# Issuing the down-product weight fetches from GpSimd's queue instead of SyncE's

## The chip, the cores and the metric

The kernel runs on one core of one Trainium2 chip. The metric is the device time of one execution in microseconds (us). Five engines work side by side: TensorE (PE, matmuls, with PEld for its weight loads), VectorE (DVE), ScalarE (ACT), GpSimd (POOL) and SyncE (SP). Data moves between device memory and the on-chip buffers by DMA. A DMA is issued by one of the engines' instruction queues: the queue waits in order, first for the semaphores of the instruction at its head, then issues it; 16 DMA engines carry the transfer out, and a semaphore tells when it has landed.

## The reference

Two layers, each a half-step SwiGLU, a mixing block and a second half-step SwiGLU, on 512 tokens of width 1024; all in float32. The change concerns the last matrix product of the SwiGLU, `@ w_down`, whose inner size D_FF is 2816 (22 tiles of 128):

```python
def _swiglu(t, w_gate, w_up, w_down):
    return (jax.nn.silu(t @ w_gate) * (t @ w_up)) @ w_down

for l in range(DEPTH):
    f = _swiglu(_rmsnorm(h, ffn1_pre_g[l]), ffn1_w_gate[l], ffn1_w_up[l], ffn1_w_down[l])
    h = h + 0.5 * _rmsnorm(f, ffn1_post_g[l])
    ...
    f = _swiglu(_rmsnorm(h, ffn2_pre_g[l]), ffn2_w_gate[l], ffn2_w_up[l], ffn2_w_down[l])
    h = h + 0.5 * _rmsnorm(f, ffn2_post_g[l])
```

## The kernel before

**Precision.** Every float32 operand is split into a high part (ScalarE's cast, line 182) and a low part (VectorE's subtraction, line 183), and each product is three matmuls: high by high, high by low, low by high (lines 205 to 207 in `mm3`). One weight block of a `Unit` is two tiles of 128 rows by 512 columns, 512 KB. It is fetched into a raw buffer, split into `wh` and `wl`, and then feeds 12 matmuls of 128x512.

**The seven products.** In the four feed-forwards (two layers, `a` before and `c` after the mixing) 16 of the 22 tiles of D_FF go through a scheme of seven products in the place of eight (Strassen's, in Winograd's form): `token_products` for the gate and up matrices and `products()` for the down matrix. Down has two chunks `ci` of eight tiles, each with seven products `n`, in the order of `DOWN`, which makes 14 jobs of two units each. `BLOCKS` says which quarter of the weights a product reads. Products 2, 3, 5 and 6 need a sum of quarters: VectorE subtracts the fetched block and a kept one (line 327, tile `bt`, made by `keep`). Product 2 fetches both quarters; product 4 takes over the raw block of product 3 and fetches nothing. The other six tiles of D_FF go through `down()`, whose blocks are plain `Unit`s.

**The order of the work.** The host program `Queue` walks a list of jobs, laid out by `PLAN`, in which the down jobs alternate with gate and up jobs of the last four tiles (kinds `g` and `u`). `Queue.load_ahead` splits the blocks of the following jobs, four units ahead; each time a block has been split, `loaded()` calls `fetch_ahead()`, which issues the next fetches in the order of the jobs until the ring that the next unit's place belongs to is full. In the down stage there are two `raw` buffers, shared with the gate and up blocks, and two buffers of the ring `o`. The framework's planner then lays out each engine's instructions, mostly in the order of the program, sets the semaphores, and may let an instruction pass another on its queue that is not ready; `keep_in_program_order` forbids this for one instruction.

**The queues.** SP's queue issues nearly every transfer of the kernel: the plain `Unit` fetches (line 249), the block fetches of `BlockUnit.block` (line 297), the transposes of `turn()` (line 808), the gain rows (line 136), the saving and bringing back of the residual, and the output. POOL's queue carries three small vectors (lines 122, 123 and 156) and some copies and memsets of the mixing, among them the tile `cut` (lines 1161 and 1164).

**What a block fetch waits for.** Its instruction waits at the head of its queue until the buffer's last reader is done, which is a VectorE instruction of line 183 or 327.

Of the kernel before, what the change touches and what calls it, by code (L numbers as in the profile page):

```python
# [18 lines left out]
P = 128  # L19
# [4 lines left out]
def kernel(  # L24
# [38 lines left out]
    nc = tc.nc  # L63
# [40 lines left out]
    def stile(shape, tag, name, dt=F32R):  # L104
        return sb.tile(shape, dt, tag=tag, bufs=BUFS[tag], name=name)
# [126 lines left out]
    class Unit:  # L232


        def __init__(self, src, k0, nk, c0, ncol, name, scale=None):
            self.tags, self.place = ("wh", "wl"), "raw"
            self.src, self.k0, self.nk, self.c0, self.ncol, self.name, self.scale = src, k0, nk, c0, ncol, name, scale
            self.h = self.raw = None
# [35 lines left out]
    class BlockUnit(Unit):  # L274
# [9 lines left out]
        def __init__(self, n, src, rows, k0, nk, ncol, keep, name, place="raw"):  # L284
            super().__init__(src, k0, nk, 0, ncol, name)
            self.n, self.rows, self.keep, self.fetched, self.place = n, rows, keep, False, place
            self.heir, self.behind = None, False

        def inherits(self, un):
            un.heir, self.place = self, None  # L290
# [3 lines left out]

        def block(self, dst, b):
            r = (b[0] * self.rows + self.k0) * P
            return nc.sync.dma_start(dst, self.src[r:r + self.nk * P, b[1] * self.ncol:(b[1] + 1) * self.ncol]
                                     .rearrange("(k p) c -> p k c", p=P))

        def fetch(self):  # L300
# [309 lines left out]
    def ffn(l, src, wg, wu, wd, dst, name, spare, parked, plan, aside=None):  # L610
# [89 lines left out]
        def sums():  # L700
# [4 lines left out]
            def fp32(i, j):  # L705
                t = whole(f"x{i}{j}")
                tt(t, block(i, j, 0).bitcast(F32), block(i, j, 1).bitcast(F32), ALU.add)
                return t
# [16 lines left out]
            yield "S2"  # L725
            tt(x11, x11, x21, ALU.subtract)
            tt(s, block(0, 1, 0).bitcast(F32), s, ALU.subtract)
            yield "S3"
            tt(s, s, block(0, 1, 1).bitcast(F32), ALU.add)
            pair(4, s)  # L730
            yield "S4"
# [126 lines left out]
        def product(at, uns):  # L858
            ci, n = DOWN[at]
            first, last = ci == 0, ci == NC - 1  # L860
            if at == 0:
                RINGS["o"] = 2
                dst.begin()
            if at + 1 < len(DOWN):
                first_factor(*DOWN[at + 1])
            if first and n in (0, 2):
                st["b", SUM[n]] = [pbank("z", f"pd{name}_{n}_{e}") for e in range(2)]
            pts = st["b", SUM[n]]
            h, l = st.pop(("a", ci, n))
            opens, ends = first and n in (0, 2), last and n in (1, 4, 6)  # L870
            for un in uns:
                for e in range(2):
                    c = slice(e * P, (e + 1) * P)
                    for k in range(un.nk):
                        kk = un.k0 + k
                        mm3(pts[e][:], h[:, kk, c], l[:, kk, c], un.h[:, k], un.l[:, k], opens and kk == 0,
                            ends and kk == FC // 2 - 1, free=True)
                        yield 3 * S * PE_US
                    turn(un.k0 + e)
            if not last:  # L880
                return
            if n == 0:
                st["b", 1] = [pbank("z", f"pd{name}_1_{e}") for e in range(2)]
                for e in range(2):
                    nc.scalar.copy(st["b", 1][e][:], pts[e][:])
                return
            i, hf = TO[n]
            for e in range(2):
                f = dst.fs[2 * i + e][:, HF[hf]]
                if n in (4, 5):  # L890
                    nc.vector.tensor_tensor(f, f, pts[e][:], ALU.add)
                else:
                    nc.scalar.copy(f, pts[e][:])

        def products():

            keep = [Keep(lambda k0, ci=ci: stile([P, 2, S], "o", f"bt{name}_{ci}_{k0}", F32)[:]) for ci in range(NC)]
            had = {}
            for at, (ci, n) in enumerate(DOWN):
                w = wd[l, ci * FC * P:(ci + 1) * FC * P]  # L900
                uns = [BlockUnit(n, w, FC // 2, k, 2, S, keep[ci], f"d{name}_{ci}_{n}_{k}", ("raw", "o")[k // 2])
                       for k in range(0, FC // 2, 2)]
                for un in uns:
                    un.behind = n == 2
                if n == 4:
                    for un, of in zip(uns, had[ci, 3]):
                        un.inherits(of)
                had[ci, n] = uns
                yield uns, (lambda at=at, uns=uns: product(at, uns))
# [18 lines left out]
        def queue(what):  # L928
            kind, n = what[0], what[1]
            if kind in "gu":  # L930
                if n not in made:
                    made[n] = plain(n)
                ms = (what[2],) if what[-1] in (0, 1) and len(what) == 3 else range(2)
                uns = made[n][kind == "u"]
                run = (lambda: gates(n, uns, ms)) if kind == "g" else (lambda: ups(n, uns, ms))
                Q.add(uns if ms[0] == 0 else [], run)
            elif kind == "a":
                Q.add([], lambda: iter(first_factor(n, 0) or ()))
            elif kind == "m":
                if name == "a0":  # L940
                    Q.add([], mem_stats)
            else:
                if what not in made:
                    made[what] = products() if kind == "d" else token_products(n, kind == "U")
                for one in made[what]:
                    Q.add(*one)
                    break
# [775 lines left out]
```

## Time and profile before

| | us |
|---|---|
| median of 3 runs | 2356.36 (2354.06 to 2357.69) |
| the profiled execution | 2354.76 |
| its span, first to last instruction | 2353.0 |
| VectorE busy in the span | 1798.8 |
| ScalarE busy in the span | 1505.3 |
| POOL busy in the span | 75.5 |

The granted clock of TensorE is 0.999 of full speed over the profiled execution. The profile is read in five views, and each row names its engine, its line in the kernel, the operation, and the tiles as "out<-in" without their buffer numbers:

- the page: the busy time of each engine, the chain of work that ended last, and the groups of transfers with the median time from issue to landing
- the busy time of each engine in stretches of the span
- the waits: who waited for whom, with the sum, the count and the longest
- the instructions on one tile, with their durations and, for transfers, the quickest, median and slowest landing
- the timeline of one engine: start, length, the instruction, and in brackets how long the engine stood idle before it and what ended that

"SPq" marks an issue on SP's queue. A PE instruction's end is modelled, so matmuls overlap in the timeline.

### The profile page before, as it was taken

Reading aid. Unit: us, or ns where it says so; the run is one execution under the profiler, and the core shown is the slowest. Engines: PE = TensorE matmul, PEld = TensorE weight load, DVE = VectorE, ACT = ScalarE, POOL = GpSimd, SP = SyncE. Lnnn points to the kernel's source line nnn. Section 1 sums busy time; section 2 is a strip of 40 time slices with the busy share of each in tenths; the row PEclk is TensorE's granted clock in tenths of the full one; section 3 lists DMA queues with packets and bytes.
Section 4 is the critical chain, followed back from the end, with each engine's and each line's share of the span. In section 5 each row is a group of like instructions: output and inputs, shape, how many; then the busy total and the mean of one; then the engine's idle time right before and its main releaser. Section 6 shows DMA issues by size and latency. Waiting matters only on the chain.

```text
span 2353.0 us, 30931 instructions
## 1 busy us (share of the span) xinstructions
PE 2339.6 (99%) x11623; PEld 1977.7 (84%) x11623; DVE 1798.8 (76%) x2359; ACT 1505.3 (64%) x2302; POOL 75.5 (3%) x134
## 2 busy tenths in 40 slices
PE   9999999999999999999999999999999999999998
PEld 7888888888888888878898888888888888988887
DVE  8877876577777688878798788766677767888785
ACT  6677465576766556774656774655777665667744
POOL 0000000000111000000000000000001100000000
PEclk9999999999999999999999999999999999999999
DMA  6667454223323555674646655532323235566744
GB/s 206 192 178 220 143 197 129 78 83 88 91 72 108 188 188 159 199 188 153 225 145 182 202 176 178 189 108 72 100 72 99 73 124 190 170 189 181 207 145 146
DMA packets 297849, 354.96 MB, mean 151 GB/s; under 512 B 78282, under 2 KB 189154, under 8 KB 297700
## 3 DMA queue, kind: packets, MB, share of 16 engines
q1 hardware_dynamic: 297604, 352.97, 48.8%
q8 instruction: 91, 1.49, 0.3%
q14 instruction: 58, 0.48, 0.1%
q0 software_dynamic: 96, 0.03, 0.0%
HBM read 319.39 MB, written 16.78 MB: 143 GB/s over the span
## 4 chain that ended last, share of the span: by engine, by line
PE 90%; DMA 4%; DVE 2%; ACT 2%; issue 1%; SPq 0%; DVEq 0%; ACTq 0%
PE pg L206 4%; PE pg L205 4%; PE pg L207 4%; PE pda L206 3%; PE pdc L206 3%; PE pda L205 3%; PE pda L207 3%; PE pdc L207 3%; PE pdc L205 3%; PE pb L207 1%; PE pb L206 1%; PE pb L205 1%; PE pq L205 1%; PE pq L206 1%; PE pk L207 1%
## 5 line engine op out<-in xcount | busy, mean ns | idle before, releaser
L205 PE MATMUL pg<-us_a,wh_wg 128*128 128x512 f32 x384 | 151.1, 394 | 0.0
L206 PE MATMUL pg<-us_a,wh_wg 128*128 128x512 f32 x384 | 149.9, 390 | 0.0
L207 PE MATMUL pg<-us_a,wl_wg 128*128 128x512 f32 x384 | 149.9, 390 | 0.0
L183 DVE TENSOR_TENSOR wl_da<-raw_da,wh_da 128x1024 fp32r<-128x1024 f32 x50 | 61.0, 1224 | 46.3 <-ACT wh_da L182 46.1
L183 DVE TENSOR_TENSOR wl_dc<-raw_dc,wh_dc 128x1024 fp32r<-128x1024 f32 x50 | 61.0, 1223 | 44.5 <-ACT wh_dc L182 44.4
L206 PE MATMUL pdc<-wl_dc,ahc 128*128 128x512 f32 x224 | 88.0, 393 | 1.5 <-DVE wl_dc L183 1.5
L206 PE MATMUL pda<-wl_da,aha 128*128 128x512 f32 x224 | 88.0, 393 | 0.3 <-DVE wl_da L183 0.3
L207 PE MATMUL pdc<-wh_dc,alc 128*128 128x512 f32 x224 | 87.3, 390 | 0.0
L207 PE MATMUL pda<-wh_da,ala 128*128 128x512 f32 x224 | 87.3, 390 | 0.0
L205 PE MATMUL pdc<-wh_dc,ahc 128*128 128x512 f32 x224 | 86.7, 390 | 0.4 <-ACT wh_dc L182 0.4
L205 PE MATMUL pda<-wh_da,aha 128*128 128x512 f32 x224 | 86.6, 390 | 0.0
L207 PEld LDWEIGHTS pg<-us_a,wl_wg 128*128 128x128 f32 x384 | 72.1, 188 | 15.1
L205 PEld LDWEIGHTS pg<-us_a,wh_wg 128*128 128x128 f32 x384 | 72.2, 188 | 14.1
L206 PEld LDWEIGHTS pg<-us_a,wh_wg 128*128 128x128 f32 x384 | 72.2, 188 | 14.0
L182 ACT CAST wh_da<-raw_da 128x1024 fp32r<-128x1024 f32 x50 | 52.2, 1049 | 41.5 <-DMA raw_da<-in_ffn_w_down_dram 13.6
L182 ACT CAST wh_dc<-raw_dc 128x1024 fp32r<-128x1024 f32 x50 | 52.1, 1049 | 36.5 <-DMA raw_dc<-in_ffn_w_down_dram 12.2
L186 DVE SCALAR_TENSOR_TENSOR wl_wg<-raw_wg,wh_wg 128x1024 fp32r<-128x1024 f32 x48 | 58.5, 1222 | 21.9 <-ACT wh_wg L185 21.8
L200 DVE SCALAR_TENSOR_TENSOR ga<-pg,bgate,ga 128x512 f32<-128x512 f32 x48 | 35.9, 747 | 50.0 <-ACT ga L199 50.0
L182 ACT CAST wh_uc<-raw_uc 128x1024 fp32r<-128x1024 f32 x44 | 46.3, 1053 | 39.8 <-PE pwc0g L207 9.4
L183 DVE TENSOR_TENSOR wl_uc<-raw_uc,wh_uc 128x1024 fp32r<-128x1024 f32 x44 | 53.7, 1221 | 17.1 <-ACT wh_uc L182 16.9
L185 ACT ACTIVATE wh_wg<-raw_wg 128x1024 fp32r<-128x1024 f32 x48 | 50.5, 1056 | 25.1 <-PE pv L1113 11.7
L182 ACT CAST wh_ua<-raw_ua 128x1024 fp32r<-128x1024 f32 x44 | 46.2, 1052 | 31.1 <-PE pwa0g L207 8.1
(643 smaller groups left out, 8017.3 us busy)
## 6 DMA issues: line engine op xcount, KB each, us to landing
raw_da<-in_ffn_w_down_dram SPq DMA_DIRECT2D x66, 512.0 KB, 4.7
raw_dc<-in_ffn_w_down_dram SPq DMA_DIRECT2D x66, 512.0 KB, 4.3
raw_ga<-in_ffn_w_gate_dram SPq DMA_DIRECT2D x52, 512.0 KB, 4.5
raw_ua<-in_ffn_w_up_dram SPq DMA_DIRECT2D x52, 512.0 KB, 4.7
raw_gc<-in_ffn_w_gate_dram SPq DMA_DIRECT2D x52, 512.0 KB, 4.0
raw_uc<-in_ffn_w_up_dram SPq DMA_DIRECT2D x52, 512.0 KB, 4.0
raw_wg<-in_w_gate_dram SPq DMA_DIRECT2D x48, 512.0 KB, 3.6
raw_wo<-in_w_out_dram SPq DMA_DIRECT2D x24, 512.0 KB, 3.4
```

Of the source, the lines that this page charges most:

```text
L182: both = [nc.scalar.copy(h_ap, src)]
L183: make = lambda: nc.vector.tensor_tensor(l_ap, src, h_ap.bitcast(F32), ALU.subtract)
L185: both = [nc.scalar.activation(h_ap, src, AF.Copy, scale=scale)]
L186: make = lambda: nc.vector.scalar_tensor_tensor(l_ap, src, scale, h_ap.bitcast(F32), ALU.mult, ALU.subtract)
L200: nc.vector.scalar_tensor_tensor(t, z, minus, t, ALU.max, ALU.add)
L205: nc.tensor.matmul(pt, lh, rh, start=start, stop=False, skip_group_check=free)
L206: nc.tensor.matmul(pt, lh, rl, start=False, stop=False, skip_group_check=free)
L207: nc.tensor.matmul(pt, ll, rh, start=False, stop=stop, skip_group_check=free)
```

## The change

`BlockUnit` gets an attribute `queue`, by default SyncE's, and `block()` issues its DMA there. `products()` sets it to GpSimd's for all units of the 14 down jobs. This covers the raw fetches and the fetches of the kept blocks of product 2, which stay pinned in program order. The gate and up products, the plain units of `down()` and everything else stay with SyncE.

```diff
@@ class BlockUnit, __init__
-            self.heir, self.behind = None, False
+            self.heir, self.behind, self.queue = None, False, nc.sync
@@ class BlockUnit, block
-            return nc.sync.dma_start(dst, self.src[r:r + self.nk * P, b[1] * self.ncol:(b[1] + 1) * self.ncol]
+            return self.queue.dma_start(dst, self.src[r:r + self.nk * P, b[1] * self.ncol:(b[1] + 1) * self.ncol]
                                      .rearrange("(k p) c -> p k c", p=P))
@@ products()
                 for un in uns:
-                    un.behind = n == 2
+                    un.behind, un.queue = n == 2, nc.gpsimd
```

## The prediction

> **What bounds the kernel now.** I read the page first, then the busy time of the four stretches in which the seven-product down jobs feed TensorE, then TensorE's waits, then the timelines of the places where a down fetch is needed soon after it lands. The page's first lines say that TensorE is the bound.
>
> ```profile
> span 2353.0 us, 30931 instructions
> PE 2339.6 (99%) x11623; PEld 1977.7 (84%) x11623; DVE 1798.8 (76%) x2359; ACT 1505.3 (64%) x2302; POOL 75.5 (3%) x134
> ```
>
> TensorE lacks 13.4 us of a full span, and all that any change can win from waiting lies in these and in what the modelled ends of matmuls hide. The next rows are of the view of busy time by stretch (start:end, length, then busy time and count for PE, PEld, DVE, ACT, POOL, then clock, DMA share, GB/s): the second of the four down stages, then the sum over all four. The last row is TensorE's longest kind of wait there.
>
> ```profile
> 1019.70:1147.00 127.30, 126.16 (x553) 103.43 (x553) 99.77 (x94) 75.80 (x85) 0.00 (x0) 1.00 0.60 180
> sum 506.20, PE 504.03 PEld 413.69 DVE 398.96 ACT 303.30 POOL 5.42; mean PE 126.01 PEld 103.42 DVE 99.74 ACT 75.83 POOL 1.36
> PE pdc L206 <- DVE wl_dc L183: 1.5, 2, 0.8
> ```
>
> In the four stages TensorE is idle for 506.20 - 504.03 = 2.2 us. Matmuls start 0.23 us apart (126.16 us for 553) and are drawn 0.39 us long, as the rows below show, so a wait hides up to 0.16 us more: with some five waits the stages lose about 3 us. **That is the ceiling of the direct gain**, 0.13% of the time; the direct loss has no such ceiling. Beside it VectorE is busy 399 of 506 us and the DMA engines 0.6 of the time, so a late weight is made good only as far as it had lead.
>
> **What is moved.** Line 297 issues each block fetch; in products() it makes 24 raw fetches per feed-forward (14 jobs of two units, less the two jobs n = 4 that inherit) and 4 for the kept blocks.
>
> ```profile
> L297 SPq DMA_DIRECT2D raw_dc<-in_ffn_w_down_dram x48: 367/368/634, 994.8 to 2290.0; - x48
> L297 SPq DMA_DIRECT2D btc<-in_ffn_w_down_dram x8: 462/487/1375, 1014.6 to 2227.0; - x8
> DMA to landing us min/median/max: 3.2/4.3/8.3
> ```
>
> So 2 x (48 + 8) = 112 issues of 512 KB leave SP, 48 x 0.37 + 8 x 0.49 = 22 us of SP's time for one name and 43 us for both. SP is no engine that TensorE waits for by itself, and I cost these 43 us at nothing: what matters is only when a fetch starts and lands. Bytes, buffers and the work of VectorE and ScalarE are the same.
>
> **The new price of one fetch.** No row shows a 512 KB fetch from POOL's queue. The nearest are the two small vectors that go that way, in POOL's timeline, with ScalarE's instruction that released the first, and the page's times from issue to landing beside two stores from SP:
>
> ```profile
> 206.13 0.63 POOL L1161 MEMSET cut<- 128x640 f32 x1 [181.52 <-ACT hra L811]
> 206.84 1.55 POOL L1164 TENSOR_SCALAR_AFFINE_SELECT cut<-cut 128x129 f32<-128x129 f32 x2
> 211.19 0.55 POOL L122 DMA_DIRECT2D vecs<-in_mem_norm_g_dram  x1 [2.80 <-ACT hra L811]
> 211.72 0.55 POOL L123 DMA_DIRECT2D vecs<-in_b_gate_dram  x1
> ```
> ```profile
> 208.35 2.54 ACT L811 COPY hra<-tra0u 128x1024 uint16<-128x1024 uint16 x2
> ```
> ```profile
> hsave<-hfa SPq DMA_DIRECT2D x8, 512.0 KB, 2.7
> gsave<-ga SPq DMA_DIRECT2D x16, 256.0 KB, 2.1
> vecs<-in_b_gate_dram POOLq DMA_DIRECT2D x1, 24.0 KB, 3.0
> vecs<-in_mem_norm_g_dram POOLq DMA_DIRECT2D x1, 4.0 KB, 3.4
> ```
>
> Two stores that differ by 256 KB differ by 0.6 us, so 512 KB take about 1.2 us to move, and SP's quickest fetch (3.2 us) has a fixed part of 2.0 us. POOL's vectors, with next to nothing to move, take 3.0 and 3.4 us: 1.0 to 1.4 us more. To this comes POOL's start: 211.19 is 0.30 us after ScalarE's end (208.35 + 2.54 = 210.89). **I take 1.5 us later per fetch** (1.2 + 0.3). Below, it could be -0.5: SP's fetches take up to 8.3 us in traffic, and the vectors, issued in the same stage, may have stood 2 us in it. Above, POOL needs 0.55 us for the 8 rows of one vector and the same 0.55 for the 48 of the other, which says that rows cost little; if those 0.55 us were all rows (48), 256 rows would take 2.9 us and a fetch would come 1.5 + 2.4 = 3.9 us later. The value nearest to the rows is the flat one, 1.5; I keep -0.5 and 3.9 as ends. The Trainium skill, DMA: Bandwidth & Descriptors, section Specifications, has a first byte after about 1 us on the GpSimd path and 0.6 us on the SyncE path; as an estimate from that page alone the fetch would be 0.4 us later and the loss below would be 0.2 us. The vectors' 3.0 us against SP's 2.0 us speak for more than that.
>
> **Where a later landing reaches TensorE.** Early in each stage the blocks land long before use. It is tight where a raw buffer comes free late. Place A is the second block of job (1,2): VectorE waits for its landing, works without a pause, and ends the low part just ahead of the second matmul (L206) that reads it. Shown are VectorE's low part and that matmul in the first a-stage and the first c-stage, and both with VectorE's wait in the last c-stage:
>
> ```profile
> 235.95 1.22 DVE L183 TENSOR_TENSOR wl_da<-bta,wh_da 128x1024 fp32r<-128x1024 f32 x1
> ```
> ```profile
> 238.45 0.39 PE L206 MATMUL pda<-wl_da,aha 128*128 128x512 f32 x1
> ```
> ```profile
> 1071.29 1.22 DVE L183 TENSOR_TENSOR wl_dc<-btc,wh_dc 128x1024 fp32r<-128x1024 f32 x1
> ```
> ```profile
> 1073.59 0.39 PE L206 MATMUL pdc<-wl_dc,ahc 128*128 128x512 f32 x1
> ```
> ```profile
> 2234.96 1.23 DVE L327 TENSOR_TENSOR btc<-btc,raw_dc 128x1024 f32<-128x1024 f32 x1 [1.44 <-DMA raw_dc<-in_ffn_w_down_dram]
> ...
> 2238.37 1.22 DVE L183 TENSOR_TENSOR wl_dc<-btc,wh_dc 128x1024 fp32r<-128x1024 f32 x1
> ```
> ```profile
> 2239.82 0.39 PE L206 MATMUL pdc<-wl_dc,ahc 128*128 128x512 f32 x1
> ```
>
> Lead is the matmul's start less the low part's end: 238.45 - 237.17 = 1.28 us, 1073.59 - 1072.51 = 1.08, 2239.82 - 2239.59 = 0.23. I take the second a-stage as the first.
>
> Place B is job (1,3). Again VectorE stands until a block lands (2.55 us in the last stage) and then has no pause before the low part:
>
> ```profile
> 2255.60 1.22 DVE L327 TENSOR_TENSOR btc<-raw_dc,btc 128x1024 f32<-128x1024 f32 x1 [2.55 <-DMA raw_dc<-in_ffn_w_down_dram]
> ...
> 2262.42 2.35 DVE L183 TENSOR_TENSOR wl_dc<-btc,wh_dc 128x1024 fp32r<-128x1024 f32 x2
> ```
> ```profile
> 2264.32 0.39 PE L206 MATMUL pdc<-wl_dc,ahc 128*128 128x512 f32 x1
> ```
> ```profile
> 1096.19 2.35 DVE L183 TENSOR_TENSOR wl_dc<-btc,wh_dc 128x1024 fp32r<-128x1024 f32 x2
> ```
> ```profile
> 1098.07 0.39 PE L206 MATMUL pdc<-wl_dc,ahc 128*128 128x512 f32 x1
> ```
>
> The first of the two low parts ends 1.22 us after the start: leads 2264.32 - 2263.64 = 0.68 us and 1098.07 - 1097.41 = 0.66 us; in the a-stages I count no loss here up to 1.5 us. Place C is job (1,5) of the last stage alone:
>
> ```profile
> 2288.72 1.23 DVE L327 TENSOR_TENSOR btc<-raw_dc,btc 128x1024 f32<-128x1024 f32 x1 [3.04 <-DMA raw_dc<-in_ffn_w_down_dram]
> 2289.87 2.35 DVE L183 TENSOR_TENSOR wl_dc<-raw_dc,wh_dc 128x1024 fp32r<-128x1024 f32 x2
> ```
> ```profile
> 2291.72 0.39 PE L206 MATMUL pdc<-wl_dc,ahc 128*128 128x512 f32 x1
> ```
>
> Its lead is 2291.72 - 2291.09 = 0.63 us.
>
> With 1.5 us later the loss is: A 0.22 + 0.22 + 0.42 + 1.27 = 2.1, B 0.84 + 0.82 = 1.7, C 0.87, together **4.7 us**. These losses add up, since a stalled matmul frees the next buffers as much later. At 2.5 us later they are A 6.1, B 3.6 (a-stages counted at nothing, for want of a row), C 1.9, together 11.6 us; at 3.9 us A 11.7, B 6.5, C 3.3, together 21.5; at -0.5 none.
>
> **What may come back.** In the first c-stage ScalarE waits for a transposed tile whose transfer SP issued just after a down fetch, and the wh casts and TensorE come after it:
>
> ```profile
> 1038.41 0.53 SPq L297 DMA_DIRECT2D raw_dc<-in_ffn_w_down_dram  x1
> 1038.99 1.39 SPq L808 DMA_TRANSPOSE trc0u<-thc0u  x1
> ```
> ```profile
> 1044.69 1.36 ACT L811 COPY hrc<-trc0u 128x1024 uint16<-128x1024 uint16 x1 [0.35 <-DMA trc0u<-thc0u]
> ```
>
> Off SP, the fetch no longer stands ahead of the transpose (0.53 us of issue and about 1.2 us of data), and a down fetch no longer stands behind a transpose or a gate fetch that waits for its own buffer. I count half of the 3 us ceiling, 1.5 us. POOL's own queue holds little: `cut` (206.13 to 208.39) and the two vectors (to 212.27) stand there in the first stage, waiting for ScalarE. A fetch queued behind the last of them would land at 212.27 + 4.3 + 1.5 = 218.1, against VectorE's first use of a block of job (0,2) here:
>
> ```profile
> 216.86 1.22 DVE L327 TENSOR_TENSOR bta<-bta,raw_da 128x1024 f32<-128x1024 f32 x1
> ```
>
> That is 1.2 us late in the worst case, once, and I count nothing for it. **Sum**: +4.7 - 1.5 = +3.2 us on the profiled execution's 2354.76 us (span 2353.0 and 1.8 around it), 2358.0. The median of the runs shown, 2356.36, is 1.6 us above that execution, so on the median's scale I predict **2359 us**, +0.1%. About 0.2% (4.7 us) is what a measurement of this kernel can tell from no change.
>
> **The rivals.**
> *Slow generation, ends slower.* POOL writes the 256 rows of a fetch at a cost per row and each fetch lands 2.5 to 3.9 us later. Places A, B and C then cost 11.6 to 21.5 us: 2366 to 2378, 2370 as a middle. It decides for slower from about 2 us later on. For it: at place A SP issues fetch behind fetch, three in 1.75 us,
>
> ```profile
> 2227.94 1.75 SPq L297 DMA_DIRECT2D raw_dc<-in_ffn_w_down_dram  x3
> ```
>
> and POOL would be slower than that. Against it: 0.55 us for 8 as for 48 rows. Chance 0.24.
>
> *VectorE holds POOL off, ends slower.* If POOL could prepare a fetch only between VectorE's instructions, the hold would be up to 1.22 us, in 399/506 = 0.79 of the time: at most 1.0 us on average, so 2.5 us later in all and 11.6 - 1.5 = 10 us, 2366. The two vectors say nothing on it, since they were issued in a pause of VectorE, whose next instruction in that stage is this:
>
> ```profile
> 212.31 1.23 DVE L183 TENSOR_TENSOR wl_da<-raw_da,wh_da 128x1024 fp32r<-128x1024 f32 x1 [4.07 <-ACT wh_da L182]
> ```
>
> Chance 0.06. The Trainium skill, SBUF — State Buffer, section SBUF: two separate sides, warns of exactly this: while VectorE runs a two-port mode, GpSimd cannot write its descriptors. The down stages hold two-input operations of 1.22 us for 1024 elements, and the section Who interferes with whom gives those no two-port mode; no run here shows it yet.
>
> *A buffer taken out of turn, ends slower.* The order on each queue is made by the program's planner. Down blocks and gate and up blocks share the two raw buffers; on an empty queue a down fetch could be placed ahead of a gate fetch that SP would have served first. The two fetches of one gate pair stand 16 us apart already:
>
> ```profile
> 230.24 0.37 SPq L249 DMA_DIRECT2D raw_ga<-in_ffn_w_gate_dram  x1
> ```
> ```profile
> 246.67 0.37 SPq L249 DMA_DIRECT2D raw_ga<-in_ffn_w_gate_dram  x1
> ```
>
> One such exchange in each stage, half of it covered by the lead that the second fetch has, is 4 x 8 = 32 us: 2391. The wait of a gate fetch for its buffer is there; that the order would turn is not. Chance 0.12.
>
> *The held queue was the limit, ends faster.* If all of the 3 us in the stages come back, fetches are no later (-0.5), and the freer SP also helps some of the 13.4 us elsewhere, the time is 2350. Against it: TensorE has too little idle time there. Chance 0.13.
>
> **How the numbers follow.** My forecast, within 0.2%, has 0.45. The slower rivals have 0.24 + 0.06 + 0.12 = 0.42 and the faster one 0.13. The range goes from 2350 (the faster case) to 2378 (fetches 3.9 us later), leaving out the exchange of buffers and the outermost gain.
>
> **What would show it.** After the change line 297's down fetches stand on POOL, 112 of them, and the page's software queue carries about 59 MB. Their time to landing should be 1.5 us above before's at the quickest (4.7 against 3.2 us). VectorE's waits for raw_dc at places A, B and C should grow, and TensorE's waits on wl_da and wl_dc from 2 to about 6 us. The wait at 1047 us of the first c-stage should shrink. If TensorE's waits grow by over 10 us, generation is slow, or VectorE holds it; if gate weights become late, a buffer was taken out of turn; if the stages are shorter than now, the held queue was the limit.

## The result, and the profile after

The changed kernel takes 2371.61 us (median; 2369.59 to 2373.36), the kernel before, run beside it, 2356.48 us (2354.06 to 2359.56). The ratio is 1.0065, with a 95% interval of 1.0054 to 1.0077: **slower by 15 us**, where the prediction had 2359 us and "within 0.2%" as the likeliest case. The time lies inside the predicted range, but none of the four rivals says how it came about. The profiled execution took 2373.27 us (before 2354.76).

The changed kernel's page, its head and busy times; then the group of `raw_dc` fetches on GpSimd, their landing, and the software queue:

```profile
span 2371.2 us, 31011 instructions
PE 2345.2 (99%) x11623; PEld 1980.1 (84%) x11623; DVE 1797.6 (76%) x2359; ACT 1505.3 (63%) x2302; POOL 156.5 (7%) x246
```
```profile
L297 POOL DMA_DIRECT2D raw_dc<-in_ffn_w_down_dram x48: 722/722/727, 1001.8 to 2308.3; - x48
DMA to landing us min/median/max: 3.7/4.2/7.8
q0 software_dynamic: 16224, 58.76, 7.6%
```

The span is 18.2 us longer (2371.2 - 2353.0). The change was made as described: 58.76 MB run in the software queue, as foreseen. But a fetch of `raw_dc` lands in 3.7, 4.2 and 7.8 us (quickest, median, slowest) against 3.2, 4.3 and 8.3 us before, where the row also counts the 18 fetches of the plain units. So a fetch from GpSimd is 0.5 us later at its quickest and no later at the median, and its issue is longer (0.72 us instead of 0.37). Only the eight kept blocks `bta` land clearly later, after 6.9 us at the median instead of 5.4.

The time went into the four down stages. Busy time by stretch, the second stage and the sum over the four, cut at the same instructions as before:

```profile
1025.90:1158.90 133.00, 129.40 (x555) 105.44 (x554) 101.93 (x97) 78.11 (x87) 15.29 (x22) 0.97 0.59 182
sum 523.40, PE 509.43 PEld 416.45 DVE 403.14 ACT 308.40 POOL 66.18; mean PE 127.36 PEld 104.11 DVE 100.78 ACT 77.10 POOL 16.55
```

They last 523.40 us instead of 506.20: 17.2 of the 18.2 us. TensorE's waits (in all, how often, the longest) name the place:

```profile
PE pdc L205 <- ACT pdc L885: 6.4, 2, 3.5
PE pda L205 <- ACT pda L885: 6.2, 2, 3.3
...
PE pdc L206 <- DVE wl_dc L183: 0.6, 1, 0.6
PE pda L206 <- DVE wl_da L183: 0.6, 1, 0.6
```

Four waits of some 3.2 us, one in each stage, 12.6 us in all, and all for one thing: the copies of line 885, with which ScalarE starts the sums of product 1 from those of product 0. They were in no list of before. The waits for the low parts (`wl_da`, `wl_dc`), for which the prediction had forecast a rise from 2 to about 6 us, fell from 1.5 + 0.3 to 0.6 + 0.6 us. After two of the four stalls TensorE also ran at half its clock for a while (PEclk is the column after the five engines). In the second stage:

```profile
1049.00:1051.90 2.90, 0.00 (x0) 0.00 (x0) 1.40 (x2) 2.90 (x5) 0.00 (x0) 0.90 0.91 193
1051.90:1054.40 2.50, 2.46 (x6) 1.97 (x7) 0.96 (x1) 2.50 (x3) 2.37 (x4) 0.50 0.60 137
1054.40:1058.20 3.80, 3.80 (x11) 2.93 (x10) 0.00 (x0) 2.57 (x4) 0.51 (x1) 0.50 0.89 324
```

In 2.9 us no matmul starts; then 17 (6 + 11) take 6.3 us, where 17 at 0.23 us would take 3.9: 2.4 us more. In the first stage it is shorter:

```profile
211.90:213.60 1.70, 1.64 (x4) 1.35 (x5) 1.06 (x1) 1.70 (x4) 1.56 (x3) 0.50 0.12 14
213.60:215.30 1.70, 1.70 (x6) 1.32 (x5) 0.00 (x0) 1.70 (x2) 1.31 (x2) 0.57 0.77 282
```

Ten matmuls take 3.4 us instead of 2.3. Stalls and half clock make 12.6 + 2.4 + 1.1 = 16.1 of the 17.2 us.

**Why the copies are late.** ScalarE's timeline ahead of them in the first stage, before and after:

```profile
203.25 1.04 ACT L182 CAST wh_da<-raw_da 128x1024 fp32r<-128x1024 f32 x1
204.21 0.58 ACT L885 COPY pda<-pda 128x512 f32<-128x512 f32 x1
204.72 1.35 ACT L811 COPY hra<-tra0u 128x1024 uint16<-128x1024 uint16 x1
205.94 1.04 ACT L182 CAST wh_da<-raw_da 128x1024 fp32r<-128x1024 f32 x1
206.88 0.58 ACT L885 COPY pda<-pda 128x512 f32<-128x512 f32 x1
```
```profile
208.24 1.33 ACT L811 COPY hra<-tra0u 128x1024 uint16<-128x1024 uint16 x1 [2.08 <-DMA tra0u<-tha0u]
209.45 1.98 ACT L182 CAST wh_da<-raw_da 128x1024 fp32r<-128x1024 f32 x2
211.33 1.06 ACT L885 COPY pda<-pda 128x512 f32<-128x512 f32 x2
```

Two things differ. **The order**: before, ScalarE did cast, L885, L811, cast, L885; now the planner has put L811 first, then both casts, then both copies. No line of the diff touches that; the planner laid out ScalarE's and VectorE's instructions anew, and SyncE's remaining ones in a few places, when the fetches left SP. **The wait**: L811 copies out a tile that a DMA has transposed, and ScalarE stood 2.08 us for that. The transposes land later than they did. A product's result is transposed as two halves, its planes; those of product (1,1) are issued beside down fetches, a little ahead of the stage. The first of these two, as ScalarE saw it in the first stage, before and after:

```profile
175.07 1.36 ACT L811 COPY hra<-tra0u 128x1024 uint16<-128x1024 uint16 x1 [0.42 <-DMA tra0u<-tha0u]
```
```profile
179.46 1.35 ACT L811 COPY hra<-tra0u 128x1024 uint16<-128x1024 uint16 x1 [3.77 <-DMA tra0u<-tha0u]
```

And SP's queue before, then SP's and POOL's after, at that place:

```profile
172.00 1.23 SPq L808 DMA_TRANSPOSE tra0u<-tha0u  x1
173.34 1.79 SPq L297 DMA_DIRECT2D raw_da<-in_ffn_w_down_dram  x2
```
```profile
173.05 1.23 SPq L808 DMA_TRANSPOSE tra0u<-tha0u  x1
```
```profile
173.64 0.72 POOL L297 DMA_DIRECT2D raw_da<-in_ffn_w_down_dram  x1 [7.39 <-DVE wl_ua L183]
```

Before, the fetch stood behind the transpose on one queue and was issued when that had been issued (173.34 against 172.00 + 1.23). Now its issue begins at 173.64, while that of the transpose still runs (173.05 + 1.23 = 174.28), and both are under way until the transpose lands. The trace's packets show what is late. In both kernels the transpose's data, 1024 packets of 256 bytes, run from 1.2 to 2.6 us after its issue. Before, it counts as landed 0.5 us after the last of them; now 3.8 us after, and the fetch's packets fill that time. For all 64 transposes (line 808), who waited for them, and the landing times of those whose landing the trace has (46 before, 48 after):

```profile
  ACT hrc L811: 15.1, 13
  ACT hra L811: 14.9, 13
```
```profile
DMA to landing us min/median/max: 3.0/3.6/6.6
```
```profile
  ACT hra L811: 21.6, 12
  ACT hrc L811: 19.9, 11
```
```profile
DMA to landing us min/median/max: 3.0/4.5/8.2
```

ScalarE's waits for transposes grew from 15.1 + 14.9 = 30.0 to 21.6 + 19.9 = 41.5 us. This sum is the measure of the experiments below.

### The profile page after: what moved, and what is told of

Read it like the earlier page. It is cut to its first block, busy times and chain, and to the rows that moved or that the text cites. A ratio compares the mean times of both kernels' runs of the same rounds, so it can differ in the third digit from the quotient of the medians.

```text
span 2371.2 us, 31011 instructions
## 1 busy us (share of the span) xinstructions
PE 2345.2 (99%) x11623; PEld 1980.1 (84%) x11623; DVE 1797.6 (76%) x2359; ACT 1505.3 (63%) x2302; POOL 156.5 (7%) x246
## 3 DMA queue, kind: packets, MB, share of 16 engines
q0 software_dynamic: 16224, 58.76, 7.6%
## 4 chain that ended last, share of the span: by engine, by line
PE 85%; DMA 5%; ACT 4%; DVE 4%; issue 2%; SPq 0%; DVEq 0%; ACTq 0%
PE pg L206 4%; PE pg L205 4%; PE pg L207 4%; PE pdc L206 3%; PE pda L206 3%; PE pdc L205 3%; PE pda L205 3%; PE pdc L207 3%; PE pda L207 3%; PE pq L206 1%; PE pq L205 1%; PE pb L207 1%; PE pq L207 1%; PE pk L206 1%; PE pk L207 1%
## 5 line engine op out<-in xcount | busy, mean ns | idle before, releaser
L297 POOL DMA_DIRECT2D raw_dc<-in_ffn_w_down_dram x48 | 34.7, 723 | 731.5 <-DVE wl_uc L183 573.4
L297 POOL DMA_DIRECT2D raw_da<-in_ffn_w_down_dram x48 | 34.7, 724 | 554.5 <-DVE wl_ua L183 401.9
```

The costliest lines, as they stand in the source:

```text
L297: return self.queue.dma_start(dst, self.src[r:r + self.nk * P, b[1] * self.ncol:(b[1] + 1) * self.ncol] .rearrange("(k p) c -> p k c", p=P))
```

## The experiments

Two theories stood at the start: **O**, the new order on ScalarE and VectorE, and **S**, the sharing of the DMA engines, by which transposes land late. The rival was what the prediction had priced: a later landing at the later jobs (places A, B, C). To part O from S, a kernel's instructions were held to another kernel's order on an engine, by dependencies without a wait from each instruction to the one that is to stand ahead of it (`ORDERS` holds the numbers of the instructions in the wanted order):

```diff
+def pin(nc, tc):
+    ...
+            tc.add_manual_dep(i, prev.name, nosync, reason="pin")
...
     with tile.TileContext(nc) as tc:
         tile_macaron_trunk_kernel(tc, *args)
+        pin(nc, tc)
```

All results in one table; "us" is the ratio to the kernel before on the same chip, applied to 2355 us; the last column is the change in ScalarE's waits for transposes against the 30.0 us above, in the profiled execution.

| run | fetches on GpSimd | order | ratio (95%) | us | waits |
|---|---|---|---|---|---|
| the change | all 112 | its own | 1.0065 (1.0054 to 1.0077) | +15.3 | +11.5 |
| e1 | all | as before | 1.0032 (1.0020 to 1.0043) | +7.5 | +7.1 |
| e2 | none | as after | 1.0030 (1.0020 to 1.0039) | +7.1 | +1.3 |
| e3 | n = 0, 1 (32) | its own | 1.0115 (1.0101 to 1.0129) | +27.1 | +13.0 |
| e4 | n = 2, 3, 5, 6 (80) | its own | 1.0006 (0.9997 to 1.0014) | +1.4 | +1.6 |
| e5 | none, two moved on SP | as before | 1.0008 (1.0000 to 1.0017) | +1.9 | +4.0 |
| e6 | all but 8 | as before | 1.0048 (1.0034 to 1.0063) | +11.3 | +2.5 |
| e7 | all | after, but five instructions | 1.0052 (1.0039 to 1.0064) | +12.2 | +3.2 |
| e8 | n = 0, 1 | as before | 1.0081 (1.0068 to 1.0094) | +19.1 | +18.0 |
| e9 | none, ScalarE 5.4 us more work | as before | 1.0024 (1.0014 to 1.0035) | +5.7 | +0.1 |
| e10 | none, ScalarE 10.9 us more work | as before | 1.0046 (1.0034 to 1.0059) | +10.8 | -0.4 |
| e11 | all but n = 1 | as before | 1.0011 (1.0002 to 1.0020) | +2.6 | +4.9 |
| e12 | all but n = 0 | as before | 1.0048 (1.0036 to 1.0061) | +11.3 | +11.9 |

**e1 and e2: order and queue apart.** `pin` holds ScalarE and VectorE; TensorE's order was the same in all. SyncE's remaining issues follow: they stand as before in e1 and as in the change in e2, so "order" takes in those few places too.

> The changed kernel (fetches on GpSimd's queue), with the order of the instructions on ScalarE and VectorE held to that of the kernel before. Theory O (order): the loss comes from the planner's new order, in which ScalarE does two casts and the copy L811 of a transposed tile ahead of the copies L885 that product (0,1) needs; with the old order the four stalls of 3.1 to 3.6 us before L885 and the two drops of the clock (about 5 us) go: 2355 to 2359 us. Theory S (sharing): the transposes land late because GpSimd's fetches share the DMA engines with them (6.39 us instead of 3.05), whatever the order, and ScalarE stands behind them: 2366 to 2373 us, with the waits for L885 still 2 us or more in each of the four stages.

> The mirror: the kernel before (fetches on SyncE's queue), with the order of the instructions on ScalarE and VectorE held to that of the changed kernel. Theory O (order): 2368 to 2374 us, with four waits of 3 us for L885. Theory S (sharing): 2355 to 2359 us, since the transposes land as early as before, and no wait for L885 above 1 us. If each is half of it: 2360 to 2366 us.

Measured: 2362.08 us (e1) and 2360.57 us (e2) against 2354.32 us. Neither theory alone: each accounts for half, and 7.5 + 7.1 = 14.6 us is nearly the whole 15.3. TensorE's waits for L885, in e1 and in e2:

```profile
PE pdc L205 <- ACT pdc L885: 0.9, 2, 0.5
PE pda L205 <- ACT pda L885: 0.9, 2, 0.5
```
```profile
PE pda L205 <- ACT pda L885: 2.7, 2, 1.6
PE pdc L205 <- ACT pdc L885: 2.7, 2, 1.5
```

With the new order and no fetch on GpSimd there are four stalls of some 1.4 us and no drop of the clock in the stages; with the fetches on GpSimd as well they grow to 3.2 us and the clock drops. The sizes fit two delays that stand one behind the other on ScalarE.

**e3 and e4: which fetches.**

```diff
-    un.behind, un.queue = n == 2, nc.gpsimd
+    un.behind, un.queue = n == 2, nc.gpsimd if n < 2 else nc.sync   # e3
+    un.behind, un.queue = n == 2, nc.sync if n < 2 else nc.gpsimd   # e4
```

> Only the fetches of the products n = 0 and n = 1 (the first four jobs of a stage) are issued from GpSimd, 32 of 112; the rest stay on SyncE. If the loss sits where the first jobs are fetched (theories O and S alike): 2367 to 2373 us, and the four waits for L885 as in the changed kernel. If it were the price of a later landing at the later jobs, or of a buffer taken out of turn, it would be 2355 to 2359 us.

> The complement: only the fetches of the products n = 2, 3, 5 and 6 are issued from GpSimd, 80 of 112 with those of the kept blocks. Theories O and S: no wait for L885, 2354 to 2359 us. If the price of a fetch at the later jobs were the loss: 2364 to 2373 us.

Measured: 2381.82 us and 2356.12 us against 2354.32. **The prediction's own price falls here**: 80 fetches, among them every one at A, B and C, cost 1.4 us (-0.7 to 3.3), not 4.7 and not 11. The loss is with the 32 fetches of the first four jobs, which run beside the transposes. That they alone cost more than all 112 was in no expectation; e8 comes back to it.

**e5 and e6: does the fetch that overtakes do it?**

```diff
     SP's order in each stage, e5 (all fetches on SyncE):
-    transpose of (1,1) first plane;  raw_d (1,0) second half
+    raw_d (1,0) second half;  transpose of (1,1) first plane
-    transpose of (1,0) first plane;  raw_d (1,1) first half
+    raw_d (1,1) first half;  transpose of (1,0) first plane
```
```diff
+    nc.sync if (ci, n, un.k0) in ((1, 0, 2), (1, 1, 0)) else nc.gpsimd   # e6
```

> The kernel before, all fetches on SyncE, the orders of ScalarE, VectorE and SyncE held to those before, except that in each down stage two fetches stand one place earlier on SyncE, ahead of a transpose instead of behind it: block (1,0), second half, ahead of the transpose at 172 us, and block (1,1), first half, ahead of the one at 202 us. No work of GpSimd is in it. Theory F (first come): what delays a transpose on the changed kernel is that a fetch gets to the DMA engines ahead of it, so the two transposes land 2 to 3 us later here too, ScalarE falls behind, and the time is 2359 to 2364 us. Theory G (the software queue): the delay belongs to GpSimd's fetches, and an exchange on one queue costs no more than the 0.4 us of an issue: 2353 to 2357 us.

> The kernel of e1 (fetches on GpSimd, ScalarE and VectorE in the order before), but these same two fetches of each stage, 8 of 112, stay on SyncE behind their transposes, and SyncE's order is held too. Theory F: the first transpose lands after 3 us again, and the loss of e1 (about 7 us) goes for the most part: 2354 to 2358 us. Theory G: 104 fetches are still GpSimd's, and little changes: 2359 to 2363 us. Other fetches of the first jobs also run beside transposes; if they matter as much as the two, the result is between, 2357 to 2360 us.

Measured: 2356.95 us (e5) and 2365.84 us (e6) against 2354.68. Theory F, first come first served, fails in its times: the same exchange within SP's queue costs 1.9 us (0 to 4.0), and taking it back on the changed kernel brings nothing. What it says of the first transpose holds. In e5, with no fetch on GpSimd, SP's queue and then ScalarE's waits for the two planes are:

```profile
173.40 0.37 SPq L297 DMA_DIRECT2D raw_da<-in_ffn_w_down_dram  x1
173.86 1.23 SPq L808 DMA_TRANSPOSE tra0u<-tha0u  x1
```
```profile
180.13 1.36 ACT L811 COPY hra<-tra0u 128x1024 uint16<-128x1024 uint16 x1 [4.40 <-DMA tra0u<-tha0u]
184.58 1.37 ACT L811 COPY hra<-tra0u 128x1024 uint16<-128x1024 uint16 x1 [0.75 <-DMA tra0u<-tha0u]
```

In this stage the first lands as late as in the change (6.25 us after its issue against 6.39), so a fetch from the same queue does this too; but ScalarE then waits 0.75 us for the second instead of 3.00 before. In e6 the first lands after 3.2 us, as forecast, and the wait for the second is 4.04 us. e6's executions scatter, 2359.66 to 2371.71 us, and its profile is of the fastest, so that its waits (+2.5 us) don't speak for its median; what the others hold is open.

**e7: five instructions of the order.**

```diff
     ScalarE in each stage:
-    L811, cast, cast, L885, L885
+    cast, L885, L811, cast, L885
```

> The changed kernel with the orders of ScalarE and VectorE held to its own, except for five instructions of ScalarE in each stage, which stand as before: cast, L885, L811, cast, L885 instead of L811, cast, cast, L885, L885. If these are all of theory O, the waits for L885 fall from 3.1 to 3.6 us to about 0.5 us, the clock does not drop, and the time is that of e1, 2359 to 2364 us. If the other 100 lines in which the orders differ carry the loss: 2368 to 2372 us.

Measured: 2365.70 us against 2354.68. The waits for L885 fell from 12.6 to 4.0 us, nearly to what was forecast, and the clock of the profiled execution is 0.999 against 0.997; but the ratio, 1.0052, is only 0.13% below that of the change, the intervals overlap, and the time lies between the two guesses. The five instructions are a part of the order's price; the rest is spread over other differences that were not taken apart.

**e8: e3 in the old order.** The edit is e3's, with `pin`.

> The kernel of e3 (only the first four jobs of a stage on GpSimd, 2381.8 us) with ScalarE's and VectorE's order held to that of before. If the loss of the queue sits in the first jobs alone and e3's excess is the planner's order: 2359 to 2365 us, like e1. If e3's excess comes from SyncE's own queue, on which a fetch of a kept block now stands between transposes that land after up to 10 us: 2370 us or more.

Measured: 2375.28 us against 2354.68: the order gives back 8 of e3's 27 us, and 19.1 remain, nearly all of it ScalarE's waits for transposes (+18.0). This lies in the second guess's range, and SyncE does issue the fetch of a kept block between the last transposes here, at 202.71 us in the first stage, where before it stood behind them. No run takes that alone away, so that it is the cause is not shown. TensorE waits here for the casts behind those transposes:

```profile
PE pdc L205 <- ACT wh_dc L182: 9.3, 2, 7.1
PE pda L205 <- ACT wh_da L182: 4.2, 2, 2.3
```

**e9 and e10: ScalarE late, and nothing else.** All on SyncE, all orders as before; the copy L811 of one tile in each stage is done once or twice more.

```diff
-    nc.scalar.copy(r[:, :, i * S + kk:(i + 1) * S:2]...
+    for again in range(2 if kk and nm.endswith("u_1_1") else 1): nc.scalar.copy(r[:, :, i * S + kk:(i + 1) * S:2]...
```

> The kernel before (no fetch on GpSimd), all orders as before, with the copy L811 of the second transposed tile of product (1,1) done twice, so that ScalarE comes out of that place 1.36 us later in each of the four stages; nothing else differs. Theory L (lateness of ScalarE is all that matters): the changed kernels lose because ScalarE is some 2 us late at L885 and the casts; 1.36 us then give about 2 to 4 us in all, 2356 to 2359 us. If the lateness of ScalarE were taken up by slack and the loss came from the fetches themselves: 2353 to 2356 us.

> The same with two extra copies, 2.7 us per stage. Theory L: slightly more than e1 (2 us per stage), 2361 to 2368 us, with waits of 1 to 2 us for L885 in each stage and perhaps a drop of TensorE's clock behind them. Without theory L: 2353 to 2357 us.

Measured: 2360.49 and 2365.84 us against 2354.97: 5.5 and 10.9 us for 4 x 1.36 = 5.4 and 4 x 2.72 = 10.9 us of ScalarE's time. **At this place of a stage each microsecond by which ScalarE falls behind is a microsecond of the kernel**, though ScalarE is busy 64% of the span. (e9's profiled execution has a drop of the clock too, mean 0.998; e10's has none.) Theory L held; for one copy its size was set too low (2 to 4 us), and the waits for L885 in e10 are only 0.5 us each where 1 to 2 were forecast, more standing at the casts and the low parts.

**e11 and e12: product 0 or product 1.**

```diff
+    un.behind, un.queue = n == 2, nc.gpsimd if n != 1 else nc.sync   # e11
+    un.behind, un.queue = n == 2, nc.gpsimd if n != 0 else nc.sync   # e12
```

> The kernel of e1 (ScalarE and VectorE in the order before), with the fetches of product n = 1 back on SyncE, those of n = 0 and of the later products on GpSimd (96 of 112). If each fetch that shares the DMA engines with the transposes does its part: about half of e1's loss, 2357 to 2360 us. If the fetches of n = 0, which run beside the first two transposes, do all: 2360 to 2364 us.

> The same with the fetches of n = 0 on SyncE instead and those of n = 1 and of the later products on GpSimd (96 of 112). Half of e1's loss, 2357 to 2360 us, if each does its part; 2354 to 2357 us, if the fetches of n = 0 do all.

Measured: 2356.97 and 2366.76 us against 2354.97, in e12 far above both guesses, in e11 at the lower edge of "half": the fetches of product 1 carry most of the loss. With those of product 0 on GpSimd as well (e1) it is rather less than without them (e12), though the intervals just overlap. The landing of the transposes in e11 and in e12:

```profile
DMA to landing us min/median/max: 3.0/3.8/6.4
```
```profile
DMA to landing us min/median/max: 3.0/4.4/11.4
```

The slowest in e12 is the second transpose of the first stage. SP's issue, two of POOL's fetches around it, and ScalarE behind it:

```profile
175.60 1.23 SPq L808 DMA_TRANSPOSE tra0u<-tha0u  x1
```
```profile
174.45 0.75 POOL L297 DMA_DIRECT2D raw_da<-in_ffn_w_down_dram  x1 [150.62 <-DVE tua L327]
178.04 0.72 POOL L297 DMA_DIRECT2D raw_da<-in_ffn_w_down_dram  x1 [2.84 <-DVE wl_ua L183]
```
```profile
187.00 1.35 ACT L811 COPY hra<-tra0u 128x1024 uint16<-128x1024 uint16 x1 [8.62 <-DMA tra0u<-tha0u]
```

Issued at 175.60 us, landed at 187.0: 11.4 us for 256 KB, with these two and a third of GpSimd's fetches (`bta`, issued at 180.04) under way, and one of SyncE's (`raw_ua`, 175.03) just ahead. ScalarE's waits for the two planes of product (1,1), added over the four stages, part the runs:

| us | first plane | second plane |
|---|---|---|
| before | 1.7 | 12.2 |
| the change | 9.6 | 10.7 |
| e1 | 8.8 | 13.3 |
| e5 | 13.1 | 3.4 |
| e6 | 1.9 | 14.2 |
| e11 | 9.5 | 9.2 |
| e12 | 1.7 | 23.7 |

In e11 product 0's fetch makes the first plane late, in e12 product 1's make the second late. Where the second comes sooner after a late first one (e5, e11), much of the delay is made good; a late second plane (e12) is not.

**What the column of waits says.** Where the order is held to before's, the time roughly follows ScalarE's waits for transposes plus its added work: e1 7.1 and 7.5 us, e8 18.0 and 19.1, e9 5.5 and 5.7, e10 10.5 and 10.8, e12 11.9 and 11.3, with e5 and e11 2.1 and 2.3 us off, and e6 as said. The waits are of one execution, and e8's is its slowest, 23.2 us above the kernel before, so there 5 us are left over. e4, in an order of its own, has 1.6 and 1.4. The kernels in the new order, or nearer to it (the change, e2, e3, e7), lie 4 to 14 us above their waits.

## Why the prediction was right or wrong

- **The number: inside the range by luck.** The forecast was +0.1%, the result +0.65%. The range's upper end, 2378 us, stands for fetches that land 3.9 us later and stall TensorE at A, B and C, and that did not happen. (The rival's lower end, 2366 us, takes off the 1.5 us that come back and 2378 us does not; with them it is 2376.)
- **"What bounds the kernel now": right.** TensorE bounds it, the ceiling of the gain is 3 us, and the loss has no ceiling. The stages lost 17.2 us.
- **"SP is no engine that TensorE waits for ... I cost these 43 us at nothing": right** as a price of the issues: in e4 80 of them left SP and nothing was gained.
- **"I take 1.5 us later per fetch": mis-sized.** The part of the start was right: POOL's issue stands 0.31 us behind VectorE's end (163.27 against 161.74 + 1.22 = 162.96), as the 0.30 us of the vectors said:

```profile
163.27 0.75 POOL L297 DMA_DIRECT2D raw_da<-in_ffn_w_down_dram  x1 [138.41 <-DVE wl_ua L183]
```
```profile
161.74 1.22 DVE L183 TENSOR_TENSOR wl_ua<-raw_ua,wh_ua 128x1024 fp32r<-128x1024 f32 x1
```

  The 1.2 us from the vectors' landing did not carry over: `raw_dc` lands at the quickest after 3.7 us, not 4.7, and its median went from 4.3 to 4.2. What made the vectors slow is not shown. The prediction's estimate from the Trainium skill, DMA: Bandwidth & Descriptors, section Specifications, was 0.4 us later; the trace agrees with it at the quickest (0.5 us) and shows no difference at the median.
- **Places A, B and C, 4.7 us: wrong, nothing came of it** (e4; in the change, the waits on the low parts fell). With landings no later at the median the leads were not used up: VectorE's waits for down blocks in that part of the last stage went from 8.1 to 6.9 us.
- **"What may come back", 1.5 us: this is the step that failed.** It saw that a fetch would no longer stand behind a transpose and booked that as a gain. The other side, that the transposes then have fetches beside them and land later, was not in the sum: ScalarE's waits for transposes grew by 11.5 us, and with the order held this side alone costs 7.5 us (e1).
- **"The work of VectorE and ScalarE are the same": right of the work, wrong of its order.** The prediction named the planner as a rival, but looked for it among the buffers (a gate fetch served late, 32 us). TensorE waits at most 0.4 us for a gate weight; the planner turned ScalarE's copies instead, and the new order costs 7.1 us (e2).
- **POOL's own queue at nothing: right.** `cut` and the vectors came later and no wait of TensorE names them.
- **The rivals.** Slow generation: no; 0.72 us per fetch, and no later landing at the median. VectorE holds POOL off: no; with VectorE busy 403 of 523 us, an issue of `raw_dc` takes 722 ns at the least and at the median and 727 at the most. Of the two-port trap that the prediction cited from the Trainium skill, SBUF — State Buffer, section SBUF: two separate sides, no run here shows anything. The held queue was the limit: no (e4).
- **The wait at 1047 us** of the first c-stage is gone, as foreseen, but TensorE now stands 3.5 us a little earlier, so this shows no gain.

## What to carry to other kernels

A queue is also an order: before a transfer is moved off a shared queue, list what stood in front of it and what stood behind, and ask for each small transfer that an engine waits for what it will now run beside. Read the engine that waits for it too: an engine that is 64% busy can be, at one place of a stage, the one on which every microsecond counts, and a copy of one of its instructions measures that directly. Where a planner lays out the program, the first thing to compare after an edit is the order on the engines that were not edited, and holding that order fixed parts the edit from its echo.

## What the runs showed of the hardware

- **A transpose beside a fetch** lands late, in two ways that the packets tell apart. Undisturbed, the first plane's data run from 1.2 to 2.6 us after the issue, and it counts as landed 0.5 us after the last. Behind a fetch on the same queue (e5) the data start 2.3 to 2.5 us after the issue. Beside a fetch from GpSimd (the change, e1, e11) the data run on time and only the landing is late, 1.7 to 3.8 us after the last packet. In all, transposes land after up to 8.2 us (the change) or 11.4 us (e12) instead of 6.6 us at most, at a median of 4.5 us in the change instead of 3.6. The Trainium skill, DMA: Bandwidth & Descriptors, section Queues, rings and completion order, says that each DMA engine takes the queues that it has work for in turn, a packet at a time. The packets here are unlike: the software queue's 58.76 MB in 16224 packets are 3.6 KB each, while the 64 transposes are 65536 packets of 256 bytes. By that rule a transpose's data would get a small share beside a fetch. For the first plane the trace doesn't show this; for the second plane in e12 it fits, as the data take 3.1 to 7.1 us instead of 2.2 to 2.9 before. What holds back the landing when the data are through is not shown.
- **TensorE's clock** fell to 0.50 after two of four stalls of some 3.2 us, and in e1 after two waits of only 0.8 us each, 1.3 us apart:

```profile
1051.25 0.50 PE L205 MATMUL pdc<-wh_dc,ahc 128*128 128x512 f32 x1 [0.77 <-ACT wh_dc L182]
1052.51 0.57 PE L206 MATMUL pdc<-wl_dc,ahc 128*128 128x512 f32 x1 [0.76 <-DVE wl_dc L183]
```
```profile
1049.60:1052.80 3.20, 1.67 (x6) 0.86 (x5) 1.57 (x2) 2.54 (x4) 0.00 (x0) 1.00 1.04 390
1052.80:1056.20 3.40, 3.40 (x9) 2.64 (x9) 3.40 (x4) 0.00 (x0) 0.00 (x0) 0.50 0.65 193
```

  The Trainium skill, TensorE: Matmul & The Clock Gate, Part 1, has half the clock after about one idle window of 3.4 us, which runs free of the kernel. The trace agrees on the half, and the drops last once or twice that length (3.4 us here and in the first stage of the change, 6.8 us in its second), but shorter idleness was enough (here six matmuls start in the 3.2 us ahead of the drop), and 3 us were not always: the third and fourth stage of the change had their stalls with the clock at 1.00.
- **Left open and not tried:** before, ScalarE already waits 3.00 us for the second transpose of the first stage, which SP issues at 176.46 us, when ScalarE's copy out of the first has ended (175.07 + 1.36 = 176.43). The two planes are halves of one tile; two tiles might free it, in either kernel.
